# The score product with the rotary queries' low part: 128 contraction rows in place of 64

## The chip, the cores and the metric

The kernel runs on one core of one Trainium2 chip. The metric is device microseconds of one execution, the median of three runs: 5072.67 us before (5072.15 to 5073.36).

## The reference, cut to what matters

The program is two transformer blocks in float32 over 2048 tokens of width 1024. The first has chunkwise retention, a pooling mixer, 32 experts of which each token takes four, and an embedding gate. The second has a projection, a state space layer, a latent attention of four heads, and an output projection. The change is in the scores of that attention:

```python
s = (jnp.einsum('bqhd,bkhd->bhqk', qn, k_nope) + jnp.einsum('bqhr,bkr->bhqk', qr, k_rope))
p = jax.nn.softmax(s * scale, axis=-1)
```

`qn` and `k_nope` have 128 elements per head and token. `qr` and `k_rope` are the rotated parts, 64 elements long; the rotary keys are shared by the four heads.

## The kernel before

Float32 products are made of split operands: a value is kept as a high part and a low part of 12 significant bits each, and `mm3` (lines 139 to 144) adds high times high, high times low and low times high. In `phase_att` (from line 1845) the four heads are walked one after another, each in eight blocks `b` of 256 queries, each block in two row tiles `t` of 128 queries. A row tile has four score tiles `Sc[c]` of 128 x 512, each a PSUM bank of its own ("sc0" to "sc3", one buffer each). So there are 4 x 8 x 2 x 4 = 256 score tiles.

One score tile takes five matmuls of 512 columns that accumulate in its bank. Three are `mm3` (lines 142, 143, 144: the query halves `qh`, `ql` stationary, the key halves `kh`, `kl` moving). The fourth and fifth are the rotary part. For these `krT` holds, for every key, the 64 high elements in rows 0 to 63 and the 64 low elements in rows 64 to 127. `load_q` copies the 64 rotated query rows twice into the second half of its tile, by two DMAs, and splits the whole tile on 128 rows, so that `qh[:, tr]` and `ql[:, tr]` hold the same 64 elements in both row halves. Line 1967 contracts 128 rows: high query times high key plus high query times low key. Line 1968 contracts rows 0 to 63 alone: low query times high key. It is the last of the accumulation.

After line 1968 VectorE (DVE) takes the maximum over the tile (line 1969, tile `mx`). After the four score tiles of a row tile DVE makes the negated maximum `nm` (lines 1973, 1974), ScalarE (ACT) takes the exponentials to tiles `P` (line 1979), which frees the four banks, and DVE inverts the sums (`rd`, lines 1983, 1984). Between score tiles, `step()` issues the work of the row tiles before: four transposes of `P` (line 1914, tile `tp`), the split of the result (`ph` on ACT by line 135, `pl` on DVE by line 136) and, two turns behind, the products with the values (`mm3` into tile `o`, 256 columns). A first score product of the next row tile has to wait for the exponentials that free its bank.

Beside this runs a background generator, one step at each `pump`: the state space layer (`s5_main`, from line 1702), whose eight-group rounds, four in all, each have a long scan on DVE (lines 1778 to 1807, tiles `m_t`, `m_X`, `m_q`), and then the loading of the weights for the output phase.

The order of the instructions on each engine is not the order of the source: the program is built with a scheduler that plays a timeline forward (`schedule_with_timeline_sim=True`), so the score products, the transposes, the value products and the state space layer come interleaved. Each engine then works through its list in the fixed order.

Retention in the first block has 64-row products too: `ret_s` (line 481) multiplies halves of 64 rows, sixteen matmuls in a row in the trace.

Of the kernel before, what the change touches and what calls it, by code (L numbers as in the profile page):

```python
# [22 lines left out]
PSUM = bass.MemoryType.PSUM  # L23
# [24 lines left out]
# rows that the experts' slots hold, by descending count of tokens; the loop at the end takes what is over  # L48
CAPS = [312, 304, 296, 288, 288, 280, 280, 280, 280, 272, 272, 272, 272, 264, 264, 264] + [260] * 3 + [256] * 13
NOV = 96  # L50
LE = T + 128  # rows of the list that an expert has
TR = T + 512  # rows of the halves of h1; those past T stand for places of the list that no token takes, no two alike in a slot
# [46 lines left out]
class G:  # L99
    """state of the trace; later(n, f) traces f after n more calls of pump"""  # L100
# [13 lines left out]
    def steps(self, n, gen):  # L114
        """traces the steps of a generator n pumps apart"""
        def go():
            for _ in gen:
                self.later(n, go)
                break
        go()  # L120
# [12 lines left out]
def split(S, hi, lo, src):  # L133
    """src == hi + lo, both of float32r's 12 significant bits"""
    S.nc.scalar.activation(hi, src, AF.Copy)  # L135
    S.nc.vector.tensor_tensor(lo, src, hi.bitcast(F32), op=OP.subtract)  # L136


def mm3(S, ps, a, b, start, stop):
    """float32 product of split operands: a = (hi, lo) stationary, b = (hi, lo) moving"""  # L140
    nc = S.nc
    nc.tensor.matmul(ps, a[0], b[0], start=start, stop=False)  # L142
    nc.tensor.matmul(ps, a[0], b[1], start=False, stop=False)  # L143
    nc.tensor.matmul(ps, a[1], b[0], start=False, stop=stop)  # L144


def piece(S, src, shape, g=None):
    """one 512 KiB piece of a weight, its rows times g, split; shape = free dims, product 1024"""
    nc = S.nc
    raw = S.wp.tile([128, 1024], F32, name="raw", bufs=S.wbufs[0])  # L150
    hi = S.wp.tile([128, 1024], F32R, name="whi", bufs=S.wbufs[1])
    lo = S.wp.tile([128, 1024], F32R, name="wlo", bufs=S.wbufs[1])
    n = shape[0] * shape[1]
    r, h, w = [x[:, :n].rearrange("p (a b) -> p a b", a=shape[0]) for x in (raw, hi, lo)]
    nc.sync.dma_start(r, src)
    if g is None:
        split(S, hi[:, :n], lo[:, :n], raw[:, :n])
    else:
        for k in range(shape[0]):
            nc.scalar.activation(h[:, k, :], r[:, k, :], AF.Copy, scale=g[:, k:k + 1])  # L160
            nc.vector.scalar_tensor_tensor(w[:, k, :], r[:, k, :], g[:, k:k + 1], h[:, k, :].bitcast(F32),  # L161
                                           op0=OP.mult, op1=OP.subtract)
    return h, w


def columns(S, pool, src, name, out=None, tag="colr", bufs=1):
    """a DRAM vector of 1024 elements as [128, 8], element k * 128 + p in row p"""
# [10 lines left out]
def rsqrt(S, pool, v, k, out=None, tag="rs"):  # L178
    """v ** -0.5 of a [128, k] tile by Newton's method"""
# [16 lines left out]
def squares(S, pool, x, n, out):  # L196
    """out = sums of x * x over the rows of x [128, n]"""
    junk = pool.tile([128, n], mybir.dt.bfloat16, name="sq_j", bufs=1)
    S.nc.scalar.activation(junk, x, AF.Square, accum_out=out)


def rsqrt1(S, pool, v, out=None, tag="rm"):
    """v ** -0.5 of a [128, 1] tile: three steps of Newton's method, scaled by -2, 16 and 1"""
# [17 lines left out]
def row_rstd(S, pool, x, n, eps, out=None, tag="rm"):  # L221
    """(mean(x * x) + eps) ** -0.5 over the rows of x [128, n]"""
# [8 lines left out]
def bcast_row(ap, n):  # L231
    """a DRAM vector of n elements on every partition"""
# [3 lines left out]
def transposes(S, dst, src, n):  # L236
    """dst[:, i, :] = src[:, i * 128:(i + 1) * 128] transposed, dst a PSUM tile"""
# [4 lines left out]
def trig(S, pool, pos, cos, sin):  # L242
    """cos and sin of pos * inv_freq; pos [128, 16] float, cos and sin [128, 16, 32]"""
# [7 lines left out]
def sincos(S, pool, cos, sin, ang, shape):  # L251
    """the angle is taken to [-pi, pi], then folded to [-pi/2, pi/2]"""
# [19 lines left out]
def load_positions(S, pool, positions, perm):  # L272
    """positions as floats, [128, 16]: column t holds tokens t * 128 + p, or p * 16 + t if perm"""
# [17 lines left out]
# ---------------------------------------------------------------- block 1: mixer  # L291
def phase_a(S):
    nc, A, X = S.nc, S.A, S.X
    with ExitStack() as es:
# [105 lines left out]
        def block(b):  # L400
# [89 lines left out]
            def ret_y(i, qT, k, v, sg, Sm):  # L490
# [18 lines left out]
                # group norm over each head  # L509
# [35 lines left out]
        def later_columns():  # L545
            """what the phases after the experts scale their weights with"""
# [13 lines left out]
# ---------------------------------------------------------------- block 1: output projection and router  # L560
def phase_b(S, p, hTs):
# [153 lines left out]
    # p @ ple_proj_w  # L715
# [22 lines left out]
def empty_list(S, p):  # L738
    """before any token: each place of the list has a row past T and a gate of zero; those rows are zero, and row T of xm"""
# [18 lines left out]
def sort_experts(S, scr):  # L758
    """experts by descending count, and the blocks of rows that are over their slots"""
# [38 lines left out]
    # rows over the capacity, in blocks of 128  # L798
# [16 lines left out]
    # which slot a block of the loop belongs to  # L815
# [21 lines left out]
# ---------------------------------------------------------------- block 1: experts  # L837
# A slot's first 256 rows are two blocks of its own; the rows past them share a block with those of the slots beside it.
# [4 lines left out]
def shared():  # L843
    """the slots that share a block"""
# [13 lines left out]
def gather(S, s, nb, n):  # L858
    """rows of the tokens of nb blocks of n rows, whose rows of the list are in s.ent"""
# [12 lines left out]
def fetch(S, s, entries):  # L872
    """rows of the tokens of a slot's own blocks; entries: the slot's rows of the list"""
# [34 lines left out]
def phase_c(S):  # L908
# [3 lines left out]
    with ExitStack() as es:  # L912
# [5 lines left out]
        def biases():  # L918
            # rows of the biases in the experts' order, then turned
# [41 lines left out]
        def turns(s, j):  # L961
            """X's rows turned and split, one step at a time"""
# [11 lines left out]
        def weights(src, deint, pool=None, bufs=None):  # L974
            """[128, 4 k, 256] of a weight, split; deint: columns to (parity, half)"""
# [41 lines left out]
        def down(s, e):  # L1017
            """rows of Y turned, then turned back, weighted and added to their tokens"""
# [52 lines left out]
        def down_rows(s, e):  # L1071
            """the same for two blocks of rows, with Y's rows as they come"""
# [40 lines left out]
        # rows over the capacity, 128 of one expert at a time  # L1113
# [38 lines left out]
def perm(ap):  # L1152
    """rows t * 16 + i of a [2048, n] array as [i][t, n]"""
# [3 lines left out]
def dense(S, hT, cols, acc, src, nk, done, g=None):  # L1157
    """acc[t] = hT[t].T @ src for four tiles, the weight streamed in pieces of two K tiles"""
# [12 lines left out]
# ---------------------------------------------------------------- block 1: per-layer embedding; block 2: projections  # L1171
def phase_dz(S):
    nc, A, X = S.nc, S.A, S.X
    with ExitStack() as es:
# [93 lines left out]
        def z_prep(i):  # L1268
            """h * g of the final norm goes on without the norm's factor, which is in S.rs1"""
# [30 lines left out]
        def rope(i, ps, nh, out):  # L1300
            """out = rotated ps, [128, nh * 64]"""
# [49 lines left out]
        def heads(b):  # L1351
            """queries, keys and values of four tiles, one step per group of products"""
# [116 lines left out]
# ---------------------------------------------------------------- block 2: state space layer  # L1469
# A chunk is 16 tokens, so chunk n's token i is row n of tile i. Partition rows (q, h) of half jj  # L1470
# hold the token j = 8 * jj + 7 - q of a chunk; rows (dir, p) hold the states of both directions.
def cmul(S, out, a, b, t):
    """out = a * b for (re, im) pairs of equal-shaped APs; t two scratch APs"""
# [19 lines left out]
def s5_prep(S, p):  # L1493
    """the layer's matrices, written to DRAM: Bm (tokens to state), CL (state to tokens), Kx (within a chunk)"""
# [24 lines left out]
    def expm1(x, out, less):  # L1519
        """out = exp(x) - less; x is overwritten"""  # L1520
# [14 lines left out]
    def sine(x, out):  # L1535
        """sin(x), |x| <= pi / 2"""
# [17 lines left out]
    # ai to [-pi, pi]; sine of it and of its half  # L1554
# [14 lines left out]
    # lam_bar - 1 = em * cos + (cos - 1) + i * (em + 1) * sin  # L1569
# [10 lines left out]
    # (lam_bar - 1) / lam  # L1580
# [22 lines left out]
    # a = lam ** 16 and its powers 1..8  # L1603
# [24 lines left out]
    for c8 in range(4):  # L1628
        # c of eight groups, turned to [(dir, p), g, h]
# [72 lines left out]
def s5_main(S, p):  # L1702
    """the layer itself, eight groups at a time: u (tiles of rows) to ys"""
# [32 lines left out]
    for e8 in range(4):  # L1736
# [32 lines left out]
        # states after each chunk, in scan order: 16 blocks of 8 chunks  # L1769
# [13 lines left out]
        # block n's last state takes a ** 8 of block n - 1's  # L1783
# [11 lines left out]
        # the other states of block n take a ** (k + 1) of it  # L1795
# [48 lines left out]
# ---------------------------------------------------------------- block 2: attention  # L1844
def phase_att(S):
    nc, A, X = S.nc, S.A, S.X
    scale = 192.0 ** -0.5
    with ExitStack() as es:
# [8 lines left out]
        early = dict(name="ld", tag="P", bufs=12)  # the first loads go to the tiles of P  # L1857

        def load(src, hname, lname, bufs, kw=dict(name="ld", bufs=2)):
            """loads and splits [128, 512]"""  # L1860
# [44 lines left out]
        def pv(h, b, P, rden):  # L1905
            """P.T, then V.T @ P.T of 256 queries, in eight steps; then turned back"""
# [38 lines left out]
        def step():  # L1945
            """the next turn of P, and the products two turns behind"""
# [7 lines left out]
        for h in range(4):  # L1954
            for b in range(8):
                nh, nb = (h, b + 1) if b < 7 else (h + 1, 0)
                P, rden = [], []
                for t in range(2):
# [4 lines left out]
                    for c in range(4):  # L1963
# [4 lines left out]
                        nc.tensor.matmul(Sc[c], ql[0:64, tr], krT[0:64, cs], start=False, stop=True)  # L1968
# [35 lines left out]
# ---------------------------------------------------------------- block 2: output  # L2004
# The weights stay on chip. What attention leaves time for is done beside it, in the tiles of the state space layer.
# [23 lines left out]
def w_out_row(S, k, hi, lo):  # L2029
    """row k of 128 of w_out, split"""  # L2030
# [6 lines left out]
def f_prep(S):  # L2037
    """half of the weights, and the start of the first tiles"""
# [153 lines left out]
def order(p, tags):  # L2192
    """lays the pool's tiles out in this order: (name, elements of 4 bytes, bufs[, the first to be used])"""
# [41 lines left out]
```

## Time and profile before

| | |
|---|---|
| time, median of three runs | 5072.67 us |
| profiled execution, span | 5080.3 us; the page gives no other time of its own |
| TensorE matmul (PE) busy | 4990.4 us, 98% |
| VectorE (DVE) busy | 3423.2 us, 67% |
| ScalarE (ACT) busy | 2588.4 us, 51% |
| score tiles of the attention, first to last | 3990 to 4806 us of the span |
| mean granted TensorE clock | 0.990 of 2.4 GHz |

The attention stage is 816 us long, of which PE is busy 797.7 us and DVE 569.1 us. The profile page gives for each engine the share of the span in which it ran an instruction. A matmul and its weight load (LDWEIGHTS, engine PEld) are two records; a load may lie under the matmul before it. Matmuls are pipelined, so one record may begin before the one before it has ended: the time that a matmul takes of PE's throughput is read from start to start, not from its duration. Forms are written rows*columns of the array and then partitions x elements of the moving operand.

### The profile page before, as it was taken

How to read it: one execution, taken by the hardware profiler on the slowest of the kernel's cores; microseconds unless marked ns; L12 is line 12 of the kernel's file. 1: busy time of each engine (PE TensorE's matmuls, PEld its weight loads, DVE VectorE, ACT ScalarE, POOL GpSimd, SP SyncE). 2: the span in 40 equal slices, each digit the busy share in tenths (PEclk: the TensorE clock that was granted, in tenths of full speed). 3: DMA queues.
4: the chain of work that ended last, by engine and by line, in shares of the span. 5: the costliest groups of instructions: out<-in, count | busy, mean ns of one | idle time of the engine just before them, and what ended most of it. 6: DMA issues, size and time to landing. Idle time of an engine off the chain costs nothing.

```text
span 5080.3 us, 85621 instructions
## 1 busy us (share of the span) xinstructions
PE 4990.4 (98%) x31503; PEld 4405.6 (87%) x31503; DVE 3423.2 (67%) x7271; ACT 2588.4 (51%) x4530; POOL 908.7 (18%) x910
## 2 busy tenths in 40 slices
PE   9999999899999999999999999989999999999999
PEld 7888788899999999999999999978888777777777
DVE  5666565586666667667777766666656486678586
ACT  5333344455555555555555555555545455555553
POOL 1121233011120112111311111123332200000011
PEclk9999999899999999999999999999999899999999
DMA  5232466557575767676776777766545512321143
GB/s 176 92 102 86 137 214 200 164 174 205 176 215 169 214 190 207 206 209 205 211 233 209 231 219 217 213 193 197 170 148 165 162 57 71 95 74 44 61 160 100
DMA packets 620263, 834.10 MB, mean 164 GB/s; under 512 B 76116, under 2 KB 451716, under 8 KB 619808
## 3 DMA queue, kind: packets, MB, share of 16 engines
q1 hardware_dynamic: 554976, 648.34, 40.4%
q0 software_dynamic: 64864, 180.24, 12.9%
q8 instruction: 250, 4.10, 0.3%
q14 instruction: 173, 1.42, 0.1%
HBM read 685.42 MB, written 143.02 MB: 163 GB/s over the span
## 4 chain that ended last, share of the span: by engine, by line
PE 55%; DMA 2%; DVE 1%; ACT 1%; issue 1%; POOL 0%; SPq 0%; DVEq 0%; ACTq 0%; POOLq 0%
PE acc L142 11%; PE acc L144 11%; PE acc L143 11%; PE tp L1914 2%; PE sc L1968 2%; PE tp L239 2%; PE sc L142 2%; PE o L142 1%; PE sc L144 1%; PE sc L143 1%; PE sc L1967 1%; PE oc L142 1%; PE oc L143 1%; PE oc L144 1%; PE o L143 1%; PE o L144 1%
## 5 line engine op out<-in xcount | busy, mean ns | idle before, releaser
L136 DVE TENSOR_TENSOR wlo<-raw,whi 128x1024 fp32r<-128x1024 f32 x810 | 991.3, 1224 | 621.5 <-ACT whi L135 604.6
L135 ACT ACTIVATE whi<-raw 128x1024 fp32r<-128x1024 f32 x810 | 900.8, 1113 | 874.2 <-PE acc L143 419.9
L142 PE MATMUL acc<-xTh,whi 128*128 128x256 f32 (+8 forms) x4096 | 1186.9, 290 | 1.1 <-ACT whi L135 1.1
L144 PE MATMUL acc<-xTh,wlo 128*128 128x256 f32 (+8 forms) x4096 | 1171.7, 288 | 3.1 <-DVE wlo L136 3.1
L143 PE MATMUL acc<-xTl,whi 128*128 128x256 f32 (+8 forms) x4096 | 1173.1, 287 | 0.0
L142 PEld LDWEIGHTS acc<-xTh,whi 128*128 128x128 f32 x4096 | 773.1, 189 | 4.4 <-issue 2.3
L143 PEld LDWEIGHTS acc<-xTl,whi 128*128 128x128 f32 x4096 | 773.8, 189 | 1.0 <-issue 0.5
L144 PEld LDWEIGHTS acc<-xTh,wlo 128*128 128x128 f32 x4096 | 770.0, 189 | 4.5 <-DVE wlo L136 4.3
L142 PE MATMUL acc<-whi,hTh 128*128 128x512 f32 (+1 forms) x1728 | 675.4, 399 | 6.4 <-ACT hTh L135 5.7
L143 PE MATMUL acc<-wlo,hTh 128*128 128x512 f32 (+1 forms) x1728 | 680.1, 394 | 0.5 <-DVE wlo L161 0.4
L144 PE MATMUL acc<-whi,hTl 128*128 128x512 f32 (+1 forms) x1728 | 677.7, 395 | 0.0
L142 PEld LDWEIGHTS acc<-whi,hTh 128*128 128x128 f32 x1728 | 325.2, 189 | 75.2 <-ACT hTh L135 8.0
L143 PEld LDWEIGHTS acc<-wlo,hTh 128*128 128x128 f32 x1728 | 326.3, 189 | 68.0 <-DVE wlo L161 1.8
L144 PEld LDWEIGHTS acc<-whi,hTl 128*128 128x128 f32 x1728 | 325.7, 188 | 68.1 <-DVE hTl L136 0.7
L143 PE MATMUL acc<-aTl,whi 128*128 128x280 f32 (+7 forms) x1216 | 350.1, 290 | 0.2
L142 PE MATMUL acc<-aTh,whi 128*128 128x280 f32 (+7 forms) x1216 | 350.1, 294 | 0.0
L144 PE MATMUL acc<-aTh,wlo 128*128 128x280 f32 (+7 forms) x1216 | 348.4, 291 | 0.0
L1969 DVE TENSOR_REDUCE mx<-sc 128x1 f32<-128x512 f32 x256 | 175.7, 688 | 141.1 <-PE sc L1968 140.2
L135 ACT ACTIVATE ph<-tp 128x512 fp32r<-128x512 f32 x256 | 152.7, 605 | 167.7 <-PE tp L1914 166.4
L142 PEld LDWEIGHTS acc<-aTh,whi 128*128 128x128 f32 x1216 | 226.6, 188 | 6.1 <-ACT whi L135 4.1
L143 PEld LDWEIGHTS acc<-aTl,whi 128*128 128x128 f32 x1216 | 229.0, 188 | 0.7 <-DVE aTl L136 0.7
L144 PEld LDWEIGHTS acc<-aTh,wlo 128*128 128x128 f32 x1216 | 227.4, 188 | 0.0
(618 smaller groups left out, 9722.9 us busy)
## 6 DMA issues: line engine op xcount, KB each, us to landing
raw<-expert_w_gate_up SPq DMA_DIRECT2D x512, 512.0 KB
raw<-expert_w_down SPq DMA_DIRECT2D x256, 512.0 KB
raw<-w_in SPq DMA_DIRECT2D x128, 512.0 KB
raw<-w_out SPq DMA_DIRECT2D x32, 512.0 KB
raw<-ple_gate_w SPq DMA_DIRECT2D x32, 512.0 KB
ag<-x_ag SPq DMA_DIRECT2D x16, 768.0 KB
x<-x SPq DMA_DIRECT2D x16, 512.0 KB
x_mixT<-mixst POOLq DMA_DIRECT2D x32, 256.0 KB, 3.0
```

What stands on the lines that cost most here:

```text
L135: S.nc.scalar.activation(hi, src, AF.Copy)
L136: S.nc.vector.tensor_tensor(lo, src, hi.bitcast(F32), op=OP.subtract)
L142: nc.tensor.matmul(ps, a[0], b[0], start=start, stop=False)
L143: nc.tensor.matmul(ps, a[0], b[1], start=False, stop=False)
L144: nc.tensor.matmul(ps, a[1], b[0], start=False, stop=stop)
L239: S.nc.tensor.transpose(dst[:, i, :], src[:, i * 128:(i + 1) * 128], S.ident)
L1914: nc.tensor.transpose(ps[:, kk, t, :], P[t][kt // 4][:, (kt % 4) * 128:(kt % 4 + 1) * 128], S.ident)
L1967: nc.tensor.matmul(Sc[c], qh[:, tr], krT[:, cs], start=False, stop=False)
L1968: nc.tensor.matmul(Sc[c], ql[0:64, tr], krT[0:64, cs], start=False, stop=True)
L1969: nc.vector.tensor_reduce(mx[:, c:c + 1], Sc[c], axis=AX.X, op=OP.max)
```

## The change

Line 1968 takes all 128 rows of its two operands:

```diff
                         nc.tensor.matmul(Sc[c], qh[:, tr], krT[:, cs], start=False, stop=False)
-                        nc.tensor.matmul(Sc[c], ql[0:64, tr], krT[0:64, cs], start=False, stop=True)
+                        nc.tensor.matmul(Sc[c], ql[:, tr], krT[:, cs], start=False, stop=True)
                         nc.vector.tensor_reduce(mx[:, c:c + 1], Sc[c], axis=AX.X, op=OP.max)
```

The product is now low query times high key plus low query times low key. Both tiles already hold data on all 128 rows. The rest of the diff deletes comments and docstrings, with the line numbers kept, and changes no statement.

## Rows read from the trace of the kernel before

**Rows 1.** The page: busy time, share of span and instructions by engine.

```profile
PE 4990.4 (98%) x31503; PEld 4405.6 (87%) x31503; DVE 3423.2 (67%) x7271; ACT 2588.4 (51%) x4530; POOL 908.7 (18%) x910
```

**Rows 2.** Groups by form, attention stage: count | busy us, mean ns | idle before.

```profile
L1968 PE MATMUL sc<-krT,ql 64*128 64x512 f32 x256 | 130.8, 511 | 0.0
L1967 PE MATMUL sc<-krT,qh 128*128 128x512 f32 x256 | 103.3, 404 | 0.0
```

**Rows 3.** Timeline of PE in the stage: start us, duration us, what.

```profile
4207.00 0.39 PE L144 MATMUL sc<-kh,ql 128*128 128x512 f32 x1
4207.23 0.39 PE L1967 MATMUL sc<-krT,qh 128*128 128x512 f32 x1
4207.55 0.50 PE L1968 MATMUL sc<-krT,ql 64*128 64x512 f32 x1
4207.98 0.50 PE L142 MATMUL sc<-kh,qh 128*128 128x512 f32 x1
4208.31 0.39 PE L143 MATMUL sc<-kl,qh 128*128 128x512 f32 x1
```

**Rows 4.** Timeline of PEld, the weight loads, in the same place.

```profile
4207.01 0.19 PEld L1967 LDWEIGHTS sc<-krT,qh 128*128 128x128 f32 x1
4207.55 0.18 PEld L1968 LDWEIGHTS sc<-krT,ql 64*128 64x128 f32 x1 [0.35 <-issue]
```

**Rows 5.** Timeline of PE around the 64-row products of retention.

```profile
306.17 0.40 PE L144 MATMUL acc<-whi,hTl 128*128 128x512 f32 x1
306.50 1.71 PE L481 MATMUL ret<-qT,kT 64*128 64x128 f32 x16
308.14 0.50 PE L142 MATMUL acc<-whi,hTh 128*128 128x512 f32 x1
308.48 0.39 PE L143 MATMUL acc<-wlo,hTh 128*128 128x512 f32 x1
```

**Rows 6.** Timeline of PE: four transposes, not after L1968, then after it.

```profile
4086.17 0.60 PE L1914 MATMUL tp<-ident,P 128*128 128x128 f32 x4
4086.53 0.36 PE L143 MATMUL o<-pl,vh 128*128 128x256 f32 x1
...
4090.85 0.66 PE L1914 MATMUL tp<-ident,P 128*128 128x128 f32 x4
4091.26 0.36 PE L143 MATMUL o<-pl,vh 128*128 128x256 f32 x1
```

**Rows 7.** Windows of L1968 alone: stretch, length, busy, count, PEclk, DMA, GB/s.

```profile
3990.00:4028.00 38.00, 7.83 (x11) 2.83 (x11) 0.60 0.74 210
...
4066.50:4181.25 114.75, 20.02 (x40) 7.31 (x40) 1.00 0.13 39
...
4245.00:4353.00 108.00, 19.36 (x39) 7.13 (x39) 1.00 0.09 31
...
4423.50:4530.00 106.50, 18.46 (x37) 6.76 (x37) 1.00 0.12 37
...
4589.00:4700.00 111.00, 17.99 (x36) 6.58 (x36) 1.00 0.12 37
```

**Rows 8.** Windows, four scan stretches: length, then PE, PEld, DVE, ACT, POOL busy.

```profile
4066.50:4181.25 114.75, 113.37 (x621) 83.85 (x620) 100.50 (x320) 62.73 (x152) 3.58 (x5) 1.00 0.13 39
4245.00:4353.00 108.00, 106.55 (x588) 78.38 (x586) 94.46 (x308) 57.31 (x138) 2.85 (x4) 1.00 0.09 31
4423.50:4530.00 106.50, 104.34 (x569) 76.50 (x568) 94.48 (x306) 57.32 (x139) 2.85 (x4) 1.00 0.12 37
4589.00:4700.00 111.00, 108.53 (x605) 81.38 (x604) 97.57 (x314) 60.58 (x147) 3.56 (x5) 1.00 0.12 37
```

**Rows 9.** Waits of DVE in the first scan stretch: us in total, times, longest.

```profile
DVE mx L1969 <- PE sc L1968: 9.0, 18, 0.9
DVE pl L136 <- ACT ph L135: 3.6, 9, 1.1
```

**Rows 10.** Waits of PE in the whole stage: us in total, times, longest.

```profile
PE sc L142 <- ACT P L1979: 5.5, 6, 2.4
```

## The prediction

> **What bounds the kernel now.** I read the page first: PE is busy 98% of the span and no other engine over 67% [rows 1], so a microsecond of PE's throughput should be a microsecond of the end, unless another engine is close behind in the stage in question. The changed line runs only in the attention stage, 3990 to 4806 us. There I asked for the groups by form, and two neighbours are worth setting side by side [rows 2]. Lines 1967 and 1968 have the same moving tile, the same 512 columns, the same bank. One contracts 128 rows and takes 404 ns a record, the other 64 rows and takes 511 ns. Half the rows is the dearer one.
>
> Durations of pipelined matmuls overlap, so next I read the timeline from start to start [rows 3]. A plain 512-column product gives way to the next after 0.23 us (L144 to L1967, 4207.00 to 4207.23). From L1967 to L1968 it is 0.32 (4207.23 to 4207.55), from L1968 to the next product 0.43, and from that one to its successor still 0.33. The weight loads say why [rows 4]: the load of L1968 starts at 4207.55, the same moment as its matmul, after 0.35 us without a load, whereas the load of L1967, at 4207.01, lies under the product before it. So at L1968 the overlap stops, and it stops again when the rows go back to 128.
>
> Is it the rows, or that L1968 ends an accumulation, or its operand? Retention has 64-row products with other operands [rows 5]. The 128-row product before them gives way after 0.33 instead of 0.23 (306.17 to 306.50), and the first 128-row product after them after 0.34 (308.14 to 308.48). Inside the sixteen the pace is 1.64 / 16 = 0.10 us with no stop between. The stops stand where the row count changes, at both edges, and nowhere else. That is what I take the cost to be.
>
> **The change part by part.** Removed: 64 rows as a different use of the array, 256 times, with two changes of row count each. The price of one, where another score product follows [rows 3]: (0.32 - 0.23) + (0.43 - 0.23) + (0.33 - 0.23) = 0.09 + 0.20 + 0.10 = 0.39 us. Where four transposes follow, the last term is the lengthening of the group [rows 6]: from its start to the next product 0.41 (4090.85 to 4091.26) against 0.35 or 0.36 undisturbed (4086.17 to 4086.53), so 0.05 and a tile costs 0.34. I take 0.38 for all, with 0.34 and 0.40 as ends. 256 x 0.38 = 97.3 us; the ends give 87 and 102.
>
> By the Trainium skill (TensorEngine Tiling (Array Packing), Key Properties) a change of tiling mode, not only of tile, drains TensorE. TensorE: Matmul & The Clock Gate (Single matmul latency, and Back-to-back issue gap) gives 379 ns for a lone warm product of 512 columns and 216 ns in a stream; an estimate from these is 163 ns for each drain, two a tile, 83 us in all. The trace's own 0.38 us a tile decides.
>
> The first eleven tiles run in a stretch whose mean granted clock is 0.60 [rows 7], so at 1.2 GHz for much of it. A stop there should cost between once and twice the 0.38, so up to 4.2 us more; but the stage is only starting there and its keys are still arriving, so I add nothing and keep 4 us for the low end.
>
> Added: 64 rows of low times low. The row beside it is L1967, the same shape as the new product, and in a stream it takes its 0.23 us like every other 512-column product [rows 3]: below and above, zero. The larger weight load (0.19 for 0.18 us [rows 4]) lies under the product before. No DMA, no split, no wait is added: `load_q` and the key load already fill all 128 rows, in the same instructions.
>
> Not everything reaches the end, because DVE is close behind in four stretches. The windows show where the scans of the state space layer run [rows 8]: 440.25 us long together, DVE busy 387.0 us of it, 88%, while PE is busy 433 us. They hold 40 + 39 + 37 + 36 = 152 of the score tiles [rows 7]. Taking 0.38 us a tile off each stretch leaves 99.6, 93.2, 92.4 and 97.3 us, and DVE's own work there is 100.5, 94.5, 94.5 and 97.6 [rows 8]. So DVE becomes the bound by 0.9 + 1.3 + 2.1 + 0.3 = 4.6 us, even with no idle moment left on it. It does have such moments that a faster PE does not close: in the first stretch 9.0 of its idle time ends with L1968, which PE then delivers earlier, but 3.6 us are waits for ACT's `ph` [rows 9]. Taken for four stretches that is up to 14 us; I let a third of it, 4.6 us, come through to PE, since the value products run two turns behind the split. Loss: about 9 us. Bounds: 0 and the rival below.
>
> What is late next: DVE's maximum and `nm`, then ACT's exponentials, which free the banks. PE waits for them 5.5 us in the whole stage now [rows 10].
>
> Sum: 97.3 - 9 = 88 us. Against the profiled execution that is 5080.3 - 88 = 4992 us of span. Its span is 7.6 us above the median of the runs, 0.15%, and a gain in the same place carries over as it is: 5072.67 - 88 = **4985 us**.
>
> **The rivals.** *All of it.* DVE's work has slack in its order and nothing comes back: 97 to 102 us, with the slow first tiles up to 106: 4967 to 4976 us. For it: PE waits for others hardly at all today. Against: the four sums above, which put DVE past PE.
>
> *DVE as a wall.* In the scan stretches the idle moments on DVE are links of its own chains and only part closes. Of its idle 53.2 us there (440.25 - 387.0), the share that ends with L1968 is 9.0 of 14.25 in the first stretch [rows 8, 9], so some 33.6 can close and 19.6 stay. The stretches then give 33.6 us instead of 57.8, and the 104 other tiles 39.5: 73 us, 5000 us. If none of it closes, 39.5 us and 5033. For it: 88% busy in the mean over stretches is near full. Against: most waits are for exactly the product that comes earlier.
>
> *No change.* The stop belongs not to the rows but to the end of the accumulation or to `ql`, and L1968 costs the same on 128 rows: 5073 us. Against: the retention products, and L144, which has `ql` as its weights as well and gives way after 0.23 us [rows 3]. By the Trainium skill (TensorE: Matmul & The Clock Gate, Part 3, What overlaps and what doesn't) weight loads overlap running matmuls only where the row groups differ; by that rule a full load would stop just as the half one does, and this rival would hold. The trace disagrees: plain 128-row loads lie under 128-row products, one every 0.23 us.
>
> *Slower.* The scheduler lays the lists out anew, or the old lists meet a faster PE badly, and the chain `mx`, `nm`, exponentials falls behind at each row tile, so that PE's first score product stands still. There are 64 such places. The gain of 97 us is gone at 1.5 us each, and past 1.7 us the kernel is measurably slower; at 1.9 us each, 122 us are lost and the time is 5072.67 + 122 - 97 = 5097 us. For it: the one edge where PE already waits, longest 2.4 us [rows 10]. Against: six waits in 64 places today, and two `step`s of PE work lie between the last score product and the next row tile.
>
> **How the numbers follow.** Forecast (4977 to 4996) 0.64; all of it 0.15; DVE as a wall (4997 to 5033) 0.16; no change 0.03; slower 0.02. The range from 4967 to 5012 holds the first two and the better half of the third, some 0.87 on paper; I leave it there, because the share of DVE's idle that closes is the one thing that I could only bound. What a measurement can tell from no change is 0.2%, 10 us: faster 0.95, same 0.03, slower 0.02.
>
> **What would show it.** In the profile after, L1968 has form 128*128 and a mean near 0.40 us; starts in a run of score products stand 0.23 us apart throughout, so a score tile takes 1.15 us instead of 1.53; the load of L1968 lies under L1967 and the waits on "issue" before it are gone; and the product after L1968 is back at 0.39 us. The stage is some 728 us long instead of 816. DVE is above 95% busy in the scan stretches, and PE's waits for `pl`, `nm` or the exponentials are longer by about 9 us in all. Nothing before 3990 us moves. I am wrong if the 0.43 after L1968 stays (the rows are not the cause), or if the starts close up and the stage still loses less than 60 us (DVE is a wall), or if PE's first score products wait at most row tiles.

## The result and the profile after

| | before | after |
|---|---|---|
| median of four runs each, us | 5072.41 (5069.20 to 5073.36) | 4983.19 (4978.97 to 4985.11) |
| ratio, 95% interval | | 0.9831 [0.9820, 0.9843] |
| profiled execution, span, us | 5080.3 | 4983.3 |
| start of the first score product to start of the last exponential | 3990.1 to 4805.6 | 3986.5 to 4709.8 |
| PE's waits in the stage, us | 20.1 | 33.2 |

The kernel is 89.2 us faster by the medians, 80 to 91 by the interval; the forecast was 88. Every engine works through the same list of instructions in the same order as before, so the two traces can be laid on each other instruction by instruction.

The page of after, busy time by engine; it answers to [rows 1]:

```profile
PE 4882.0 (98%) x31503; PEld 4420.4 (89%) x31503; DVE 3414.1 (69%) x7271; ACT 2588.7 (52%) x4530; POOL 901.7 (18%) x910
```

Groups by form in the stage, as in [rows 2]: L1968 now costs what L1967 costs.

```profile
L1968 PE MATMUL sc<-krT,ql 128*128 128x512 f32 x256 | 101.4, 396 | 0.0
L1967 PE MATMUL sc<-krT,qh 128*128 128x512 f32 x256 | 101.3, 396 | 0.0
```

PE's timeline, as in [rows 3]. A score tile, L1967 to L1967, takes 1.13 us:

```profile
4199.81 0.39 PE L1967 MATMUL sc<-krT,qh 128*128 128x512 f32 x1
4200.03 0.39 PE L1968 MATMUL sc<-krT,ql 128*128 128x512 f32 x1
4200.26 0.39 PE L142 MATMUL sc<-kh,qh 128*128 128x512 f32 x1
4200.49 0.39 PE L143 MATMUL sc<-kl,qh 128*128 128x512 f32 x1
4200.71 0.39 PE L144 MATMUL sc<-kh,ql 128*128 128x512 f32 x1
4200.94 0.39 PE L1967 MATMUL sc<-krT,qh 128*128 128x512 f32 x1
```

The weight loads at the same place, as in [rows 4]: the load of L1968 starts at 4199.81, with the product L1967 and so under it, 0.23 us behind the load of L1967 and with no wait on issue.

```profile
4199.58 0.19 PEld L1967 LDWEIGHTS sc<-krT,qh 128*128 128x128 f32 x1
4199.81 0.19 PEld L1968 LDWEIGHTS sc<-krT,ql 128*128 128x128 f32 x1
```

**Where the 97.0 us between the two spans lie.** I followed the start of the `mx` reductions (line 1969) through both traces.

| stretch | tiles | saved, us | 0.38 us a tile |
|---|---|---|---|
| before the first `mx` (3995.2, now 3991.2) | 0 | 4.0 | 0 |
| first to 25th `mx` | 24 | 15.6 | 9.1 |
| the next 57 row tiles | 228 | 75.0 | 86.6 |
| to the last `mx` (4801.6, now 4705.8) | 3 | 1.2 | 1.1 |
| after it | 0 | 1.2 | 0 |

What the medians do not show of the 97.0 is 7.8 us: the profiled execution of before lay that much higher above its median than that of after. The 4.0 us that stand ahead of every changed instruction belong to this; where the other 3.8 lie is not known, so the rows below are those of this pair of traces.

The first 24 tiles gained 6.5 us more than 0.38 us a tile. PE idles 1.6 us there before and 3.6 after, so it sets the pace, and its mean granted clock over the stretch is 0.82 before and 0.96 after (last section). The 57 row tiles behind them lost 11.6 us. To see where, windows over the scan rounds of the state space layer, from the first L1779 to the last L1807 of each; columns are length, then busy time of PE, PEld, DVE, ACT, POOL. After:

```profile
4049.70:4151.90 102.20, 97.41 (x612) 86.36 (x611) 97.16 (x316) 60.47 (x147) 3.66 (x6) 1.00 0.12 40
4205.70:4307.20 101.50, 98.84 (x626) 87.22 (x625) 97.37 (x321) 61.81 (x148) 3.56 (x5) 1.00 0.12 37
4365.10:4462.40 97.30, 91.21 (x573) 79.96 (x572) 93.52 (x308) 57.85 (x139) 2.85 (x4) 1.00 0.14 44
4516.90:4616.10 99.20, 94.76 (x604) 83.90 (x603) 94.87 (x312) 60.67 (x147) 3.56 (x5) 1.00 0.13 41
sum 400.20, PE 382.22 PEld 337.43 DVE 382.92 ACT 240.81 POOL 13.63; mean PE 95.56 PEld 84.36 DVE 95.73 ACT 60.20 POOL 3.41
```

The sum over the same instructions before (its bounds differ by a few us from those of [rows 8]):

```profile
sum 442.50, PE 434.92 PEld 321.84 DVE 390.77 ACT 237.95 POOL 12.84; mean PE 108.73 PEld 80.46 DVE 97.69 ACT 59.49 POOL 3.21
```

The rounds hold 152 score tiles in both. They are 42.3 us shorter, where 152 x 0.38 = 57.8 were to go. DVE's share rose from 88.3% (390.77 of 442.50) to 95.7% (382.92 of 400.20), and PE's idle time in them from 7.6 to 18.0 us.

Row tile by row tile it is sharper. Of the 57, 14 have DVE busy 97% or more after the change; before, one had. These 14 saved 0.94 us each in place of 1.52, so 8.1 of the 11.6 us are lost there. Two stretches show the contrast: two row tiles at the end of the third scan round, then three row tiles with no scan beside them. Before:

```profile
4502.75:4529.14 26.39, 25.87 (x144) 19.41 (x144) 25.15 (x64) 16.09 (x39) 0.72 (x1) 1.00 0.12 36
4768.40:4796.96 28.56, 28.56 (x149) 20.24 (x150) 15.66 (x34) 14.02 (x38) 0.71 (x1) 1.00 0.02 5
```

The same instructions after:

```profile
4437.03:4462.53 25.50, 23.25 (x144) 20.08 (x143) 25.14 (x64) 16.15 (x39) 0.72 (x1) 1.00 0.12 37
4678.55:4702.35 23.80, 23.80 (x149) 21.24 (x148) 15.38 (x33) 13.94 (x37) 0.71 (x1) 1.00 0.02 6
```

In the first, DVE has 25.14 us of work for 64 instructions on either side of the change. With that work it could not become shorter than 25.14 us; it went from 26.39 to 25.50, 0.89 us for eight score tiles instead of 3.04. In the second, DVE has a third of its time free, and twelve tiles give 4.76 us, a little over 12 x 0.38 = 4.56.

What PE waits for in the stage, us in total, times, longest. Before, beside [rows 10]:

```profile
PE tp L1914 <- DVE pl L136: 3.0, 7, 0.7
```

After, where the second line answers to [rows 10], and `ot` is the result of the value products that ACT copies out of PSUM:

```profile
PE tp L1914 <- DVE pl L136: 6.6, 14, 1.2
PE sc L142 <- ACT P L1979: 6.2, 6, 2.4
PE tp L1914 <- DVE nm L1974: 3.7, 5, 1.3
PE tp L239 <- ACT ot L1931: 2.9, 6, 0.5
```

All waits for DVE in the stage went from 5.6 to 15.6 us, those for ACT from 14.5 to 17.3. In the 57 row tiles alone PE's waits rose from 13.1 to 24.0 us: those for DVE from 3.1 to 13.1, those for ACT from 10.0 to 10.6. So 10.9 of the 11.6 us that these tiles lost stand in the trace as waits, 10.0 of them for DVE. Half of the 13.1 fall in the 14 row tiles with DVE at 97% or more, half in the other 43. The wait of the first score product for the exponentials is as rare and as long as it was.

### The profile page after: what moved, and what is told of

It is laid out like the page before. It is cut to its first block, busy times and chain, and to the rows that moved or that the text cites. A ratio compares the mean times of both kernels' runs of the same rounds, so it can differ in the third digit from the quotient of the medians.

```text
span 4983.3 us, 85621 instructions
## 1 busy us (share of the span) xinstructions
PE 4882.0 (98%) x31503; PEld 4420.4 (89%) x31503; DVE 3414.1 (69%) x7271; ACT 2588.7 (52%) x4530; POOL 901.7 (18%) x910
## 3 DMA queue, kind: packets, MB, share of 16 engines
q0 software_dynamic: 64864, 180.24, 13.1%
## 4 chain that ended last, share of the span: by engine, by line
PE 50%; DVE 5%; DMA 2%; ACT 1%; issue 1%; SPq 0%; POOL 0%; DVEq 0%; ACTq 0%; POOLq 0%
PE acc L142 12%; PE acc L143 12%; PE acc L144 12%; PE tp L239 2%; PE tp L1914 1%; PE oc L142 1%; PE oc L143 1%; PE oc L144 1%; DVE pl L136 1%; DVE mx L1969 1%; PE sc L142 1%; PE sc L143 1%; PE sc L1967 1%; PE sc L144 1%; PE sc L1968 1%
## 5 line engine op out<-in xcount | busy, mean ns | idle before, releaser
L143 PE MATMUL acc<-xTl,whi 128*128 128x256 f32 (+8 forms) x4096 | 1174.0, 287 | 0.0
L143 PEld LDWEIGHTS acc<-xTl,whi 128*128 128x128 f32 x4096 | 774.6, 189 | 1.0 <-issue 0.5
L143 PE MATMUL acc<-wlo,hTh 128*128 128x512 f32 (+1 forms) x1728 | 679.9, 394 | 0.8 <-DVE wlo L161 0.8
L143 PEld LDWEIGHTS acc<-wlo,hTh 128*128 128x128 f32 x1728 | 325.9, 189 | 68.0 <-DVE wlo L161 2.0
L143 PE MATMUL acc<-aTl,whi 128*128 128x280 f32 (+7 forms) x1216 | 350.4, 291 | 0.2
L143 PEld LDWEIGHTS acc<-aTl,whi 128*128 128x128 f32 x1216 | 229.2, 189 | 0.7 <-DVE aTl L136 0.7
L866 POOL DMA_INDIRECT rows<-x_xm,row x68 | 81.2, 1194 | 758.3 <-PE acc L144 290.4
```

The costliest lines, as they stand in the source:

```text
L866: nc.gpsimd.indirect_dma_start(out=r[:n], out_offset=None, in_=X["xm"], in_offset=bass.IndirectOffsetOnAxis(ap=s.row[:n, b:b + 1], axis=0))
```

## The experiments

The theory: the stops stand at every change between 64 and 128 rows, 0.39 us for a pair of edges; their removal is partly given back where DVE is nearly full. The rivals for the price: any row count below 128 costs it, the end of an accumulation costs it, or the 64-row product itself is slow. The rivals for what is given back: DVE's total of work, or the links `tp`, `ph`, `pl` and `mx`, `nm` that PE waits for. Ratios are against the kernel before, run beside them (medians 5074.0 for e1 to e4, 5072.0 for e5 to e7, 5071.9 for e8 to e10, 5071.6 for e11 and e12). Only e1 and e8 have their instructions in the order of the kernel after, which is that of before; in the others the scheduler laid the lists out anew. The lists of e3 and e4 are in one order, and so are those of e6 and e7, and of e10 and e12.

**e1: 96 rows in place of 128**

```diff
-  nc.tensor.matmul(Sc[c], ql[:, tr], krT[:, cs], start=False, stop=True)
+  nc.tensor.matmul(Sc[c], ql[0:96, tr], krT[0:96, cs], start=False, stop=True)
```

> Line 1968 contracts the first 96 rows of both tiles: low query times high key and half of low times low. Theory (the stop belongs to a change between a 64-row use of the array and its full use, and 96 rows need the full one): starts 0.23 us apart, as with 128 rows, 4983 us. Rival (any row count other than 128 stops the overlap): as with 64 rows, 0.32 before and 0.43 after it, 5072 us.

4990.57 us, 0.9832 [0.9815, 0.9848]. Its groups by form, and its timeline:

```profile
L1968 PE MATMUL sc<-krT,ql 96*128 96x512 f32 x256 | 102.4, 400 | 0.0
```

```profile
4202.39 0.40 PE L1967 MATMUL sc<-krT,qh 128*128 128x512 f32 x1
4202.62 0.39 PE L1968 MATMUL sc<-krT,ql 96*128 96x512 f32 x1
4202.86 0.39 PE L142 MATMUL sc<-kh,qh 128*128 128x512 f32 x1
```

No stop on either side of 96 rows: the starts are 0.23 and 0.24 apart, and the interval of the time overlaps that of the kernel after. So it is not every row count below 128. By the Trainium skill (TensorEngine Tiling (Array Packing), Available Configurations) the array can be split into tiles of 64 or of 32 rows, and 96 is not among them; the trace fits that reading, 96 rows being run as a full array.

**e2: the 64-row product first in its accumulation (made from the kernel before)**

```diff
-  mm3(S, Sc[c], (qh[:, ts], ql[:, ts]), (kh, kl), True, False)
-  nc.tensor.matmul(Sc[c], qh[:, tr], krT[:, cs], start=False, stop=False)
-  nc.tensor.matmul(Sc[c], ql[0:64, tr], krT[0:64, cs], start=False, stop=True)
+  nc.tensor.matmul(Sc[c], ql[0:64, tr], krT[0:64, cs], start=True, stop=False)
+  mm3(S, Sc[c], (qh[:, ts], ql[:, ts]), (kh, kl), False, False)
+  nc.tensor.matmul(Sc[c], qh[:, tr], krT[:, cs], start=False, stop=True)
```

> The 64-row product of the kernel before opens the accumulation of its score tile instead of ending it. Theory (cost at the two edges between 64 and 128 rows): both edges are still there, 5072 us within 15. Rival (the stop belongs to the last product of an accumulation): it moves to the rotary product of 128 rows, which now ends, and is no longer at the 64-row one; or it is gone, 4985 us.

5075.79 us, 1.0006 [0.9997, 1.0016]. Its timeline, with line 1966 the 64-row product and line 1968 the end of the accumulation before:

```profile
4211.17 0.39 PE L1968 MATMUL sc<-krT,qh 128*128 128x512 f32 x1
4211.49 0.50 PE L1966 MATMUL sc<-krT,ql 64*128 64x512 f32 x1
4211.92 0.50 PE L142 MATMUL sc<-kh,qh 128*128 128x512 f32 x1
4212.25 0.39 PE L143 MATMUL sc<-kl,qh 128*128 128x512 f32 x1
```

The same 0.32, 0.43 and 0.33 as in [rows 3], now at the start of the tile. The place in the accumulation has no part in it.

**e3 and e4: the low product twice, on 64 rows (from before) and on 128 (from after)**

```diff
   nc.tensor.matmul(Sc[c], qh[:, tr], krT[:, cs], start=False, stop=False)
+  nc.tensor.matmul(Sc[c], ql[0:64, tr], krT[0:64, cs], start=False, stop=False)  # e4: ql[:, tr], krT[:, cs]
   nc.tensor.matmul(Sc[c], ql[0:64, tr], krT[0:64, cs], start=False, stop=True)  # e4: ql[:, tr], krT[:, cs]
```

> The kernel before with its 64-row product issued twice in a row in each score tile (it counts twice in the scores). Theory (cost by edges): the second product adds its plain 0.23 us, 256 x 0.23 = 59 us, 5131 us, and it starts 0.23 us after the first. Rival (cost by 64-row product): 59 + 97 more, 5228 us.

> The kernel after with its 128-row low product issued twice in each score tile (it counts twice in the scores); its lists have the same order as those of the 64-row product issued twice. Theory by edges: 4983 + 59, less up to 12 us that PE lost to waits for VectorE and that now have more cover: 5030 to 5042 us, some 90 to 100 us below the 64-row twin. Rival by product: the same time here, but 190 us below the twin.

e3: 5148.22 us, 1.0144 [1.0127, 1.0161]. e4: 5052.28 us, 0.9961 [0.9949, 0.9974]. The timeline of e3, with lines 1968 and 1969 the two 64-row products:

```profile
4206.22 0.50 PE L1968 MATMUL sc<-krT,ql 64*128 64x512 f32 x1
4206.55 0.39 PE L1969 MATMUL sc<-krT,ql 64*128 64x512 f32 x1
4206.88 0.50 PE L142 MATMUL sc<-kh,qh 128*128 128x512 f32 x1
4207.22 0.39 PE L143 MATMUL sc<-kl,qh 128*128 128x512 f32 x1
...
4207.68 0.39 PE L1967 MATMUL sc<-krT,qh 128*128 128x512 f32 x1
4208.00 0.50 PE L1968 MATMUL sc<-krT,ql 64*128 64x512 f32 x1
4208.34 0.39 PE L1969 MATMUL sc<-krT,ql 64*128 64x512 f32 x1
```

The second 64-row product takes 0.39 us where the first takes 0.50: what follows a change of row count is slow, not what has 64 rows. It starts 0.33 or 0.34 us after the first, not 0.23 as I had expected. The pair shows how a change is paid: the product before it gives way some 0.09 us late (starts 0.32 and 0.33 apart), the product behind it some 0.11 late (0.33 and 0.34), on the way in as on the way out. Over the two places shown, from L1967 past both low products to L143, that makes 0.32 + 0.33 + 0.33 + 0.34 = 1.32 us, 0.40 more than four times 0.23, where a single 64-row product costs 0.39.

The two kernels differ by 95.9 us. Had each 64-row product its own price, that would be some 190; for one pair of edges a tile 97 was expected. The second product itself cost more than 256 x 0.23 = 59 us in both: 74 in e3 and 66 to 69 in e4, which lies 10 us above its expected range. In e4 I had expected the added PE time to cover waits; instead PE's waits in the 57 row tiles are 29.9 us, against 24.0 in after (15.2 in e3, 13.1 before). The rest of the excess is not explained.

**e5: no low product at all (from after)**

```diff
-  nc.tensor.matmul(Sc[c], qh[:, tr], krT[:, cs], start=False, stop=False)
-  nc.tensor.matmul(Sc[c], ql[:, tr], krT[:, cs], start=False, stop=True)
+  nc.tensor.matmul(Sc[c], qh[:, tr], krT[:, cs], start=False, stop=True)
```

> The product of line 1968 is left out (the low part of the rotary queries is missing from the scores). Theory (VectorE is close behind PE in the four scan stretches, so only the part of PE's time that lies outside them is still worth its full price): the 104 tiles outside give 104 x 0.23 = 24 us, the 152 inside half or less of their 35 us: 4940 to 4960 us. Rival (VectorE is no bound, PE's time is worth all of itself): 256 x 0.23 = 59 us below 4983, 4924 us or less.

4942.56 us, 0.9750 [0.9733, 0.9768]: 41 to 44 us below the kernel after, 0.16 to 0.17 us a tile of the 0.23 that were taken off PE. What PE then waits for first:

```profile
PE tp L1914 <- DVE pl L136: 12.9, 22, 1.5
PE tp L1914 <- DVE nm L1972: 7.3, 9, 1.5
```

With PE faster still, the waits for `pl` double against those of after, and 18 row tiles in place of 14 have DVE busy 97% or more. Of the 59 us taken off PE about a quarter is given back, as the theory of this run had it (4940 to 4960 us).

**e6 and e7: the scan without its last part, 64 instructions (from after, from before)**

```diff
-  nc.vector.tensor_mul(q[0], x, ak[0])
-  nc.vector.tensor_mul(q[1], y, ak[1])
-  nc.vector.tensor_tensor(q[0], q[0], q[1], op=op)
-  nc.vector.tensor_add(xv[d][:, hs, 1:16, 0:7], xv[d][:, hs, 1:16, 0:7], q[0])
```

> The kernel after without the last part of the scan (lines 1804 to 1807, 64 instructions, some 48 us of VectorE; the states within a block stay incomplete). Theory (some 12 us of the gain are lost to waits for VectorE in the scan stretches): 6 to 15 us below 4983, 4968 to 4977 us. Rival (the missing 12 us are something else): 4983 us.

> The kernel before without the same part of the scan; its lists have the order of the run above. Theory: PE with 64-row products leaves VectorE enough time, so 0 to 5 us below 5074, 5069 to 5074 us, and the distance between this and the run above is wider than 89 us, 95 to 102. Rival (VectorE's scan costs PE time in either kernel, or in neither): as much below 5074 as the run above is below 4983.

e6: 4989.57 us, 0.9837 [0.9821, 0.9854]. e7: 5073.37 us, 1.0001 [0.9991, 1.0010]. They are 84 us apart, no more than before and after, so the theory's 95 to 102 failed, and so did its 4968 to 4977 for e6: 48 us less work for DVE bought nothing. But the scheduler laid the lists out anew around the missing work. What is left of the scan rounds, from first to last scan instruction, still has DVE busy 90.6% (with the last part, in after, 93.2%); row tiles at 97% or more are 8 instead of 14; and what PE waits for in e6 moved:

```profile
PE sc L142 <- ACT P L1975: 11.3, 10, 2.7
PE tp L1910 <- DVE pl L136: 7.6, 13, 1.6
PE tp L239 <- ACT ot L1927: 5.2, 11, 0.5
```

The waits for the exponentials rose from 6.2 to 11.3 us and those for `ot` from 2.9 to 5.2. The run tells against a simple wall made of DVE's total; as a test of DVE's local load it is spoiled by the new order.

**e8, e9: the kernel after once more, and with the same cure for retention**

e8 is the kernel after, unchanged. In e9 the keys of each 64-row half lie in a tile of their own that is zero in the other half, so that the sixteen products of retention contract 128 rows (the lines that make, clear and fill these tiles are left out here):

```diff
-  r = slice((h % 2) * 64, (h % 2) * 64 + 64)
-  nc.tensor.matmul(pr[h % 2][:, h // 2, :], kT[r, h // 2, :], qT[r, h // 2, :],
+  nc.tensor.matmul(pr[h % 2][:, h // 2, :], kT[h % 2][:, h // 2, :], qT[:, h // 2, :],
```

> The kernel after once more, beside the next two on the same chip: 4983 to 4990 us.

> The kernel after, and the same remedy for the 64-row products of retention (line 481): the keys of each head half stand in a tile of their own whose other 64 rows are zero, so that all sixteen matmuls of a row tile contract 128 rows. Theory by edges: 16 row tiles x two edges x about 0.19 us = 6 us below the kernel after. The price is one more ScalarE copy of about 0.6 us a row tile beside a busy PE. Against it: the lists come out in another order, which may be worth as much either way. In the trace the sixteen start 0.23 us after the product before them instead of 0.33.

e8: 4986.41 us (4983.80 to 4987.40), 0.9824 [0.9809, 0.9838]. e9: 4982.82 us (4978.85 to 4988.20), 0.9815 [0.9801, 0.9830], no difference that can be told. The timeline of e8 at one early group of the sixteen:

```profile
145.14 1.16 PE L481 MATMUL ret<-qT,kT 64*128 64x128 f32 x16
146.23 0.50 PE L142 MATMUL acc<-whi,hTh 128*128 128x512 f32 x1
```

And of e9 at a later one:

```profile
307.10 0.39 PE L144 MATMUL acc<-whi,hTl 128*128 128x512 f32 x1
307.33 1.95 PE L488 MATMUL ret<-qT,kT 128*128 128x128 f32 x16
309.03 0.48 PE L142 MATMUL acc<-whi,hTh 128*128 128x512 f32 x1
```

The stop ahead of the sixteen is gone (0.23 us, [rows 5] has 0.33). But the sixteen take 1.70 us on 128 rows, and on 64 rows half of the groups take 1.09. From the product before a group to the second product behind it, all sixteen groups together take 40 us of PE in e9 and 34 in e8: the groups take back more than the edges give. That the whole kernel is no slower for it is not explained; all its lists are in another order.

**e10 and e12: a piece of the scan moved to POOL (from after), and the same again**

```diff
-  nc.vector.tensor_mul(t[1], y, a1[1])
+  nc.gpsimd.tensor_mul(t[1], y, a1[1])
```

> The kernel after with one of the two multiplications of the scan's first part (line 1779, 56 instructions of 0.39 us) on GpSimd instead of VectorE: 22 us less work on VectorE in the scan stretches. Theory (VectorE is the bound there): 3 to 8 us faster than the kernel after. Rival (a longer way between the engines costs as much, or GpSimd waits behind its own DMA issues): the same or slower.

> The kernel after with one multiplication of the scan on GpSimd, a second time, since its gain over the kernel after was 6.6 us with intervals that overlap: 4977 to 4982 us if that gain is there, 4984 to 4988 if it was chance.

e10: 4979.83 us (4976.53 to 4982.38), 0.9812 [0.9797, 0.9827]. e12: 4979.39 us (4977.04 to 4982.12), 0.9820 [0.9807, 0.9834]. Both lie 3 to 7 us below the two medians of the kernel after, and every run of both below every run of e8; the intervals of the ratios overlap, so the gain is likely and not proven. Row tiles with DVE at 97% or more fell from 14 to 10, but PE's waits for DVE in the 57 row tiles stayed at 13.2 us, against 13.1 in after. So the trace does not show that the gain comes from DVE. It is the fastest version here that leaves nothing out.

**e11: the low part of `P` not split off (from after)**

```diff
-  pl = p.tile([128, 2, 256], F32R, name="pl", bufs=3)
-  split(S, ph, pl, ps.rearrange("p k t q -> p k (t q)"))
-  return lambda: mult(s, ph, pl)
+  nc.scalar.activation(ph, ps.rearrange("p k t q -> p k (t q)"), AF.Copy)
+  return lambda: mult(s, ph, ph)
```

> The kernel after without the low part of the transposed weights (the subtraction of line 136 into pl is left out, 256 instructions of 0.69 us, and the value products take the high part twice; PE's work is the same). This takes away the link that PE's waits name most, transposes to pl, and 170 us of VectorE. Theory (the 12 us that the stage lost are the waits on links through VectorE, where the fixed order meets a faster PE): PE's waits for VectorE in the stage fall from 18 to under 6 us and the time by 8 to 14 us from 4986, 4972 to 4978 us. Rival (they turn into waits for ScalarE, or the loss is not in these waits): 4982 to 4990 us.

4963.61 us (4962.07 to 4965.31), 0.9788 [0.9775, 0.9802]: 23 us below e8, above the 8 to 14 expected. The longest sums of PE's waits in the stage:

```profile
PE tp L239 <- ACT ot L1930: 4.5, 9, 0.9
PE sc L142 <- ACT P L1978: 4.5, 7, 1.5
```

PE's waits for DVE in the stage fell from 15.6 to 2.0 us, in the 57 row tiles from 13.1 to nothing; those for ACT in the stage fell from 17.3 to 15.3. So the work and the links on DVE are what PE had waited for. The edit takes a link and 256 subtractions on DVE (0.69 us each) away together, and the lists come out in another order, so it does not tell these apart; and of the 23 us only about 16 are waits that the profile names. Eleven row tiles still have DVE at 97% or more, with no wait of PE for it: the share by itself does not show a wall.

## Why the prediction was right, and where it was not

**The price of the stops** was right: 0.09 + 0.20 + 0.10 us at two changes of row count. All three are gone after, they stand in e2 wherever the 64-row product stands, two 64-row products in a row cost 0.40 in e3 and not twice 0.39, and 96 rows do not have them. One reading beside it was wrong: inside the sixteen of retention I saw no stop. In that same group the second of the sixteen starts 0.21 us behind the first, and most of the others at 0.11 or less: the product behind the change is late there too. By the Trainium skill (TensorE: Matmul & The Clock Gate, Part 3, What overlaps and what doesn't) a load overlaps running products only where the row groups differ. After the change every load of a score tile uses all rows and lies under the product before, 0.23 us apart. The measurement decides against that rule here, and the rival *no change* falls with it. The estimate of 83 us from the 379 and 216 ns of the Trainium skill (TensorE: Matmul & The Clock Gate, Single matmul latency, and Back-to-back issue gap) was 14 us below the 97.3 from the trace. That section gives 216 ns as the gap of an isolated product and about 131 ns for a stream of loads and products; the stream here runs at 0.23 us, near the first.

**The first tiles** were mis-sized. I added nothing for the eleven at the low clock and kept 4 us for the low end. The first 24 tiles gave 6.5 us beyond 0.38 a tile, and what I had not thought of goes with it: the slow stretch itself became shorter. Its length differs from trace to trace (last section), so the 6.5 is luck in part.

**Not everything reaches the end** was right in kind and place, and too small. I worked out 9 us: 4.6 because DVE's work passes PE's time in the four stretches, and as much again for its own links. The trace gives 11.6 for the 57 row tiles, and in the scan rounds alone 15.5 (57.8 - 42.3), with 3.5 to 4 us above the forecast elsewhere in the stage. The step that came out too small is the comparison of averages: over a whole round DVE's work exceeded PE's new time by 0.3 to 2.1 us, but inside a round the load is uneven, and two row tiles together had DVE at 95% already before (25.15 of 26.39 us). If the order is fixed, such a stretch can only shrink to DVE's work, however much slack the next one has; that this is the way of the whole loss is argued, not shown. DVE's share of 95.7% after is what I said would show. So are the waits for `pl`, `nm` and the exponentials: together 9.0 us in the stage before and 18 after, 9 longer.

**DVE as a wall** (4997 to 5033) did not hold for the stage; 14 of 57 row tiles come near it. What of the loss is DVE's plain load and what its links stays open: e10 and e12 moved load and gained a little with PE's waits for DVE unchanged, e6 removed more and gained nothing, e11 removed both, and all four have another order.

**All of it** (4967 to 4976) was out by the 11.6 us. **Slower** did not come: the lists are the same, and PE's first score products wait 6 times and 6.2 us, against 6 times and 5.5 us.

**Nothing before 3990 moves** did not hold for this pair of traces: the first `mx` comes 4.0 us earlier. In e8's trace, of the same kernel as after, it is at 3992.9, 1.7 us later than in after, so differences of this kind come from run to run.

**The sum**: 88 forecast, 89.2 by the medians. It came out closer than its terms, and that is luck: 6.5 us more at the start stand against 2.6 more lost in the row tiles behind it, and the traces differ from the medians by 7.8 us.

## What to carry to other kernels

A lone product on half the rows between full ones costs more than the full one: read from start to start over both edges, not from its duration, and fill the rows with anything that is harmless. Where the half-row products come in a group that alternates between the halves, as in retention, full rows took more of PE's time and gained nothing that can be told. And when one engine is made faster, compare its new time with the next engine's work in windows of single tiles and not of whole rounds, and read the engine's waits there as well.

## What the runs showed of the hardware

**The clock at the start of the stage.** Windows of 5 us; after the busy times of PE, PEld, DVE, ACT and POOL comes the granted clock as a share of 2.4 GHz. Before:

```profile
3995.00:4000.00 5.00, 5.00 (x11) 2.77 (x10) 2.58 (x4) 0.54 (x1) 0.00 (x0) 0.50 1.11 353
...
4015.00:4020.00 5.00, 4.31 (x15) 2.82 (x14) 1.00 (x3) 2.29 (x6) 0.00 (x0) 0.50 0.54 88
4020.00:4025.00 5.00, 5.00 (x28) 4.27 (x26) 2.19 (x5) 4.50 (x11) 0.00 (x0) 0.85 0.02 3
```

After:

```profile
3990.00:3995.00 5.00, 5.00 (x13) 3.90 (x13) 2.58 (x4) 1.84 (x3) 0.00 (x0) 0.50 1.05 331
3995.00:4000.00 5.00, 3.46 (x19) 2.58 (x17) 1.69 (x4) 2.26 (x7) 0.00 (x0) 0.97 1.02 327
```

In both PE ran at 2.4 GHz until the stage began, waited 2.4 and 2.2 us for the first keys, and fell to 1.2 GHz within 2 us of the first score product. With the 64-row products it stayed there for about 31 us, without them for about 7, and then ran at 2.4. The other traces fit: 14 to 34 us in all at 1.2 GHz in the four kernels with 64-row score products (before, e2, e3, e7), 3 to 10 in those without. Pairs of kernels with one order of lists show what goes with it. Where the slow time was 24 us longer (before against after, e3 against e4), the first 24 tiles differed by 6.5 and 9.2 us beyond 0.38 a tile; where it was 10 us longer (e7 against e6), by 2.7. Why the clock comes back later was not tried by itself.

**Halves beside each other.** Sixteen 64-row products of 128 columns that alternate between the two halves of the rows took 1.09 us in half of the groups, 0.07 us each, against 1.70 to 1.89 in most groups on all rows, 0.11 each. In e8's trace they start two by two there, 0.01 us apart and mostly 0.11 us from pair to pair, so products of different halves ran beside each other. In the groups of 1.64 us and more most start singly, 0.11 us apart; what keeps these from pairing was not found.
